# A hybrid encoder layer on one core: the output's gate row summed in the convolution stage instead of the value stage, and ones columns set by VectorE

## The chip, the cores and the metric

The kernel runs on one core of a Trainium2 chip. The metric is the device time of one execution in microseconds. The kernel before takes 1390.58 us, the median of three runs (1390.57 to 1395.54).

The core has five engines with a queue of instructions each, and each works through its queue in order: TensorE (PE, with its weight loads PEld), VectorE (DVE), ScalarE (ACT), GpSimd (POOL) and SyncE (SP). SP, ACT and POOL also issue DMAs; an issue that has to wait for a semaphore holds up what is queued behind it on that engine. SBUF is the on-chip memory; PSUM is where TensorE's results land.

## The reference, cut to what matters

One layer over 2048 tokens of width 1024, in float32:

```
shift, scale, gate = split(silu(c) @ w_ada + b_ada, 3)
h = rmsnorm(x, norm_w) * (1 + scale) + shift
proj = h @ w_in + b_in
na_out = neighbourhood_attention(q, k, v, rpb) * silu(z)
qk = silu(conv5(concat(ml_q, ml_k)) + conv_b)
hm = mlstm(qk, ml_v, forward) + mlstm(qk, ml_v, backward), gated and normalised
x = x + gate * (concat(na_out, ml_out) @ w_out)
out = rmsnorm(x, final_norm_w)
```

What the change is about is `gate`: a row of 1024 numbers, the last third of silu(c) times w_ada (1024 x 1024 of it, 4.2 MB) plus its bias. The kernel multiplies it into the columns of w_out before the output projection.

## The kernel before, in words

Every large matmul is done as three, on a high and a low part of each operand (`mm3`, lines 426 to 431), so that float32 precision is kept. The layer goes through these stages:

- **Start** (`start`): loads x, computes shift and scale, normalises and transposes x into `hhi`/`hlo`, and does the first value projections.
- **Value stage** (`tok_blocks`, after two blocks that `start` does): weight blocks 2 to 5, of 256 columns each, times 16 tiles of 128 tokens. Blocks 2 and 3 go through `vo_group`, blocks 4 and 5 through `nav_group`, in groups of four tiles. A tile is 24 matmuls into one of four PSUM banks (`pp`). VectorE adds the bias from PSUM into a staging tile (L499 for `stvo`, L464 for `stv`), which frees the bank. There are two staging tiles, used by turns; the store of one (L506, L468) is deferred by a group. In `vo_group` a column of ones stands beside each head's values; POOL sets it by a memset at the head of a group (L488).
- **Convolution stage** (`conv_blocks`): weight blocks 6 to 9, two halves each, four tiles of 512 tokens per half, so 32 tiles of 24 matmuls. ScalarE moves a tile from PSUM into `u` (L773), VectorE runs the five taps (L806, L808) one tile later, ScalarE applies Silu (L809), SP stores the result (L813), and for the keys TensorE transposes it (L819) and ScalarE copies it out (L821).
- After these come the mLSTM with the remaining projections (`phase1b`), and the neighbourhood attention with the output projection (`phase2`).

Beside the main work of a stage runs a chain of small steps, a Python generator called `self.chain`. `next(self.chain, None)` after each tile lets it issue one step.

- In the value stage the chain is `gate_chain` (the mLSTM's gates as columns), then `decays`: for 16 groups it loads rows of `d_mneg` by a broadcast (L702), POOL adds a mask (L710), ScalarE takes the exponential (L714) and stores the result into `d_ck` (L716). `decays` has a second generator, `beside`, which it steps once per group: `gate_row`.
- `gate_row` loads eight row blocks of w_ada, 128 x 1024 (512 KB) each, into the two halves of `wide` (L401), and sums them on VectorE, each row weighted by its element of silu(c), into `gsum` (L408, L410). A matmul with a column of ones adds the 128 partitions (L418), VectorE adds the bias (L420), and the row is written to DRAM, to `d_gate`. The final norm's weights go the same way, through `wide` into `d_fnw`.
- In the convolution stage the chain is `gated_out`. It reads `d_gate` back as a broadcast over 128 partitions (L730), loads w_out in 16 halves of 128 x 512 into two buffers (L737), multiplies each by the gate (L744) and stores it in `d_wo` (L745). A half takes two steps, one per tile.

SP's queue in the convolution stage carries the weight loads (L193, `raw`), the 24 copies of table rows that `tables_rows` issues at the head of each of the first three weight blocks (L551), the stores of the convolution and `gated_out`'s loads and stores.

In the phase up to the end of the mLSTM the order of the code is not the order on the engines. The instructions are put in order when the kernel is built, by dependencies, the order of the code and an estimate of durations; the order on each engine is then fixed. The trace shows it: the first table copies (L551) of the convolution stage's first block are issued at 184.7 us. Only `phase2` has an order written out by hand.

Of the kernel before, what the change touches and what calls it, by code (L numbers as in the profile page):

```python
# [62 lines left out]
class Kernel:  # L63
# [30 lines left out]
    def scratch(self):  # L94
# [9 lines left out]
        self.d_wo = d.tile([KT, P, D], F32, name="d_wo")  # L104
        self.d_fnw = d.tile([1, D], F32, name="d_fnw")
        self.d_gate = d.tile([1, D], F32, name="d_gate")
        self.d_rneg = d.tile([NH, 15, 31], F32, name="d_rneg")
# [282 lines left out]

    def gate_row(self, pool):

        nc = self.nc
        cact = pool.tile([P, KT], F32, name="cact2")
        nc.sync.dma_start(cact, self.cT)
        nc.scalar.activation(cact, cact, AF.Silu)
        acc = pool.tile([P, D], F32, name="gsum")
        buf = [self.wide[:, :D], self.wide[:, D:]]

        def load(kt):  # L400
            nc.sync.dma_start(buf[kt % 2], self.w_ada[kt * P : (kt + 1) * P, 2 * D : 3 * D])  # L401

        load(0)
        load(1)
        yield
        for kt in range(KT):
            if kt == 0:
                nc.vector.tensor_scalar(acc, buf[0], cact[:, kt : kt + 1], None, ALU.mult)  # L408
            else:
                nc.vector.scalar_tensor_tensor(acc, buf[kt % 2], cact[:, kt : kt + 1], acc, ALU.mult, ALU.add)  # L410
            if kt + 2 < KT:
                load(kt + 2)
            yield
        row = buf[0][0:1]
        nc.sync.dma_start(row, self.b_gate)
        for j in range(2):
            ps = self.sp.tile([P, GT], F32, tag="sp", name=f"gp_{j}")
            nc.tensor.matmul(ps[0:1, :], self.ones[:, 0:1], acc[:, j * GT : (j + 1) * GT], start=True, stop=True)  # L418
            yield
            nc.vector.tensor_add(row[:, j * GT : (j + 1) * GT], row[:, j * GT : (j + 1) * GT], ps[0:1, :])  # L420
        nc.sync.dma_start(self.d_gate, row)
        row = buf[1][0:1]
        nc.sync.dma_start(row, self.fnw)
        nc.sync.dma_start(self.d_fnw, row)

    def mm3(self, ps, lhi, llo, rhi, rlo):
# [58 lines left out]
    def vo_group(self, h, slot, g, first=None):  # L485
        nc = self.nc
        st = self.stage_tile(f"stvo_{h}_{g}")
        nc.gpsimd.memset(st[:, :, 128:129], 1.0)  # L488
        brow = self.brows[h % 2]
# [67 lines left out]
    def tok_blocks(self, chain_pool):  # L557
        self.wide = chain_pool.tile([P, 2 * D], F32, name="wide")
        self.chain = itertools.chain(self.gate_chain(chain_pool, self.gates), self.decays(chain_pool, self.gate_row(chain_pool)))
        order = [2, 3, 4, 5]  # L560
        self.tables_begin(chain_pool)
        for n, blk in enumerate(order):
            self.load_w(blk + 1, (blk + 1) % 2)
            if blk < 5:
                self.load_bias(blk + 1)
            for g in range(NG):
                if blk < 4:
                    self.vo_group(blk, blk % 2, g)
                else:
                    self.nav_group(blk, blk % 2, g)  # L570
            if n > 0:
                self.tables_columns(n - 1)
        for _ in self.chain:
            pass
        self.flush()
# [108 lines left out]

    def decays(self, pool, beside):

# [21 lines left out]
        for n, (h, gi) in enumerate(groups):  # L708
# [8 lines left out]
            yield  # L717
            next(beside, None)
            yield
            if n + 2 < len(groups):  # L720
                load(n + 2)
            yield
        for _ in beside:
            pass

    def gated_out(self, pool):

        nc = self.nc
        gate = pool.tile([P, D], F32, name="gate")
        nc.sync.dma_start(gate, self.d_gate.broadcast_to([P, D]))  # L730
        halves = [(k, slice(j * GT, (j + 1) * GT)) for k in range(KT) for j in range(2)]
        raws = {}

        def load(n):
            k, cs = halves[n]
            raws[n] = pool.tile([P, GT], F32, tag="wraw", bufs=2, name=f"wraw_{n}")
            nc.sync.dma_start(raws[n], self.w_out[:, k, cs])  # L737

        load(0)
        load(1)  # L740
        yield
        for n, (k, cs) in enumerate(halves):
            raw = raws.pop(n)
            nc.vector.tensor_tensor(raw, raw, gate[:, cs], ALU.mult)  # L744
# [4 lines left out]
            yield  # L749


    def conv_blocks(self, pool):
# [4 lines left out]
        for i, (blk, kind, pair) in enumerate(order):  # L757
# [445 lines left out]
    def phase2(self):  # L1203
# [426 lines left out]
```

## Time and profile before

| | |
|---|---|
| median of three runs | 1390.58 us |
| the profiled execution | 1391.12 us |
| its span, from the first instruction to the last | 1388.9 us |
| mean granted TensorE clock | 0.983 |
| TensorE busy | 1309.5 us, 94% |
| VectorE busy | 830.7 us, 60% |
| ScalarE busy | 528.2 us, 38% |
| GpSimd busy | 292.6 us, 21% |
| moved by DMA | 263.67 MB, 190 GB/s |

In the rows of the profile a group reads: line, engine, operation, the tile it writes and those it reads, shapes and count, then busy time and the mean duration in ns, then the idle time of the engine just before these instructions and who ended it. A row of the timeline has the start and the duration in us, and in brackets the idle time before it with its releaser. A row of waits has the total, the number of waits and the longest. "SPq" and "ACTq" are DMA issues. A table of stretches has the busy time of each engine in a stretch with its number of instructions, then the granted clock, the busy share of the 16 DMA engines and the rate in GB/s.

### The profile page before, as it was taken

How to read it: one execution, taken by the hardware profiler on the slowest of the kernel's cores; microseconds unless marked ns; L12 is line 12 of the kernel's file. 1: busy time of each engine (PE TensorE's matmuls, PEld its weight loads, DVE VectorE, ACT ScalarE, POOL GpSimd, SP SyncE). 2: the span in 40 equal slices, each digit the busy share in tenths (PEclk: the TensorE clock that was granted, in tenths of full speed). 3: DMA queues.
4: the chain of work that ended last, by engine and by line, in shares of the span. 5: the costliest groups of instructions: out<-in, count | busy, mean ns of one | idle time of the engine just before them, and what ended most of it. 6: DMA issues, size and time to landing. Idle time of an engine off the chain costs nothing.

```text
span 1388.9 us, 23365 instructions
## 1 busy us (share of the span) xinstructions
PE 1309.5 (94%) x8052; PEld 1126.1 (81%) x8052; DVE 830.7 (60%) x2563; ACT 528.2 (38%) x1129; POOL 292.6 (21%) x321
## 2 busy tenths in 40 slices
PE   2989998998999999999999998999998999999996
PEld 2989998898887777888878887788876888888885
DVE  6683323111355569156867877877736777777674
ACT  4642334523222323213323313333345555555551
POOL 4453212424101010001212002212402111112111
PEclk9999999999999999999999999999999999999998
DMA  9798449788457675554776878846697897876862
GB/s 319 227 299 212 122 99 237 186 201 203 120 112 205 149 194 159 170 161 141 194 209 205 246 224 228 231 134 182 181 260 221 187 220 168 204 182 171 193 160 74
DMA packets 269707, 263.67 MB, mean 190 GB/s; under 512 B 33466, under 2 KB 230074, under 8 KB 269590
## 3 DMA queue, kind: packets, MB, share of 16 engines
q1 hardware_dynamic: 178062, 186.45, 50.5%
q0 software_dynamic: 21504, 37.73, 11.0%
q10 hardware_dynamic: 70024, 38.02, 9.7%
q8 instruction: 64, 1.05, 0.3%
q14 instruction: 53, 0.43, 0.1%
HBM read 177.57 MB, written 92.72 MB: 195 GB/s over the span
## 4 chain that ended last, share of the span: by engine, by line
PE 49%; DMA 8%; DVE 4%; issue 3%; ACT 1%; POOL 1%; POOLq 0%; ACTq 0%; SPq 0%; DVEq 0%
PE pq L865 19%; PE y L1420 10%; PE pO L1383 4%; PE pT L1368 3%; DMA tab<-d_t 2%; DMA kv<-d_ck 2%; PE pi L1093 2%; PE pc L429 2%; PE px L1091 2%; PE pc L430 2%; PE pc L431 2%; PE dc L1039 1%; PE pS L1341 1%; PE pS L1340 1%; DMA d_qna<-qst 1%
## 5 line engine op out<-in xcount | busy, mean ns | idle before, releaser
L865 PE MATMUL pq<-hhi,whi_a 128*128 128x512 f32 x512 | 208.7, 408 | 1.3 <-ACT u L773 0.8
L865 PE MATMUL pq<-hlo,whi_a 128*128 128x512 f32 x512 | 209.1, 408 | 0.0
L865 PE MATMUL pq<-hhi,wlo_a 128*128 128x512 f32 x512 | 208.4, 407 | 0.5 <-DVE wlo_a L842 0.5
L1347 ACT ACTIVATE pbuf<-pbuf,mn 128x480 f32<-128x480 f32 (+5 forms) x128 | 76.4, 598 | 105.5 <-DVE mn L1346 105.3
L865 PEld LDWEIGHTS pq<-hhi,whi_a 128*128 128x128 f32 x512 | 97.5, 190 | 19.2 <-ACT u L773 1.2
L865 PEld LDWEIGHTS pq<-hhi,wlo_a 128*128 128x128 f32 x512 | 97.5, 191 | 17.7 <-DVE wlo_a L842 1.0
L865 PEld LDWEIGHTS pq<-hlo,whi_a 128*128 128x128 f32 x512 | 97.5, 190 | 16.4
L1420 PE MATMUL y<-hhi,whi_a 128*128 128x512 f32 x256 | 85.8, 404 | 3.1 <-ACT hhi L1321 2.8
L1420 PE MATMUL y<-hhi,wlo_a 128*128 128x512 f32 x256 | 84.3, 399 | 0.0
L1346 DVE CUSTOM_DVE_ANT_0 pbuf<-pS,tab 128x480 f32<-128x480 f32 (+5 forms) x128 | 65.1, 541 | 29.3 <-PE pS L1341 19.4
L839 POOL TENSOR_TENSOR wlo_a<-rawq,whi_a 128x1024 fp32r<-128x1024 f32 x20 | 48.1, 2407 | 162.9 <-ACT whi_a L838 123.2
L1115 POOL TENSOR_TENSOR hm<-hm,ck 128x128 f32<-128x128 f32 x64 | 26.4, 412 | 263.3 <-DVE hm L1114 178.5
L429 PE MATMUL pvo<-whi_b,hhi 128*128 128x256 f32 x256 | 74.7, 292 | 7.2 <-DVE stvo L499 7.2
L1023 DVE TENSOR_SCALAR wv<-kv,gtile 128x129 f32<-128x129 f32 x120 | 37.9, 323 | 63.0 <-PE dc L1039 33.3
L1096 ACT ACTIVATE num<-px,gtile 128x129 f32<-128x129 f32 x120 | 38.3, 365 | 95.1 <-PE px L1091 75.3
L431 PE MATMUL pvo<-whi_b,hlo 128*128 128x256 f32 x256 | 73.6, 288 | 0.0
L430 PE MATMUL pvo<-wlo_b,hhi 128*128 128x256 f32 x256 | 73.6, 287 | 0.0
L499 DVE TENSOR_TENSOR stvo<-pvo,brow 128x256 f32<-128x256 f32 x64 | 26.5, 420 | 73.6 <-PE pvo L431 59.8
L714 ACT ACTIVATE dec<-dec,gtile 128x128 f32<-128x128 f32 x128 | 42.0, 392 | 69.7 <-POOL dec L710 52.2
L464 DVE TENSOR_TENSOR stv<-pv,brow 128x256 f32<-128x256 f32 x32 | 12.8, 423 | 85.4 <-DMA d_vna<-stv 38.8
L1383 PE MATMUL pO<-pt,v 128*64 128x128 f32 (+3 forms) x832 | 61.3, 283 | 0.5 <-ACT pt L1370 0.5
L1368 PE MATMUL pT<-ident,pbuf 128*128 128x128 f32 (+2 forms) x416 | 59.6, 282 | 0.0
(298 smaller groups left out, 3580.2 us busy)
## 6 DMA issues: line engine op xcount, KB each, us to landing
ck<-d_ck SPq DMA_DIRECT2D x64, 384.5 KB
kv<-d_ck SPq DMA_DIRECT2D x120, 128.5 KB
rawq<-in_w_main_dram SPq DMA_DIRECT2D x28, 512.0 KB
raw<-in_w_main_dram SPq DMA_DIRECT2D x20, 512.0 KB
d_ck<-stvo SPq DMA_DIRECT2D x16, 514.0 KB
x<-in_x_dram SPq DMA_DIRECT2D x16, 512.0 KB
wada<-in_w_ada_dram SPq DMA_DIRECT2D x32, 256.0 KB
dec<-d_mneg SPq DMA_DIRECT2D x32, 256.0 KB
```

What stands on the lines that cost most here:

```text
L429: nc.tensor.matmul(ps, lhi(k), rhi(k), start=(k == 0), stop=False)
L430: nc.tensor.matmul(ps, lhi(k), rlo(k), start=False, stop=False)
L431: nc.tensor.matmul(ps, llo(k), rhi(k), start=False, stop=(k == KT - 1))
L714: nc.scalar.activation(t[:, d, o, :], t[:, d, o, :], AF.Exp, bias=self.cols["g"][:, d, h, c : c + 1])
L839: nc.gpsimd.tensor_tensor(lo[:, :, cs], raw, hi[:, :, cs].bitcast(F32), ALU.subtract)
L865: nc.tensor.matmul(patch_ps(ps) if patch else ps, w, self.htok(h, g, k, patch), start=(k == 0 and n == 0), stop=(k == KT - 1 and n == 2))
L1096: nc.scalar.activation(num[:, d, :], px[:, d, :], AF.Copy, scale=self.cols["inter"][:, d, h, c : c + 1])
L1346: nc.vector.tensor_tensor_reduce(pt[:, :nk], ps, tabs[place[u]][j][:, :nk], 1.0, 3e38, ALU.add, ALU.min, mn)
L1347: nc.scalar.activation(pt[:, :nk], pt[:, :nk], AF.Exp, bias=mn, scale=-1.0, accum_out=sums[:, j : j + 1])
L1368: nc.tensor.transpose(ps[:cs, i, :], pts[j][:, i * cs : (i + 1) * cs], self.ident)
L1383: nc.tensor.matmul(po[j * HD : (j + 1) * HD, :], v[:n, h * HD : (h + 1) * HD], pt[j][:n, i, :], start=(i == 0), stop=(i == nch - 1))
L1420: nc.tensor.matmul(y, m[:, k, :], w[k][:, cs], start=(k == 4 and n == 0), stop=(k == 3 and n == 2))
```

## The change

`gate_row` is gone, and with it `d_gate`, `d_fnw` and the argument `beside` of `decays`. Its work is in `gated_out`, in the convolution stage: the sums are taken over halves of 512 columns, first the eight row blocks of the first half, then those of the second, each piece 128 x 512 (256 KB) in the buffers of the w_out halves. After the eighth piece of a half, a matmul with a full 128 x 128 tile of ones adds the partitions and leaves the row in all 128 of them, and VectorE adds it to `gate`, which was loaded with the bias as a broadcast. Then the 16 halves of w_out are multiplied and stored as before. The chain of the convolution stage is stepped twice per tile, before and after it; a piece of the sum takes one step, a half of w_out two. The final norm's weights are read from the kernel's input. In `vo_group` the ones columns are set by VectorE.

```diff
-    def gate_row(self, pool):
...
     def vo_group(self, h, slot, g, first=None):
-        nc.gpsimd.memset(st[:, :, 128:129], 1.0)
+        nc.vector.memset(st[:, :, 128:129], 1.0)
...
     def decays(self, pool):
             yield
-            next(beside, None)
             yield
...
     def gated_out(self, pool):
+        cact = pool.tile([P, KT], F32, name="cact2")
+        nc.sync.dma_start(cact, self.cT)
+        nc.scalar.activation(cact, cact, AF.Silu)
         gate = pool.tile([P, D], F32, name="gate")
-        nc.sync.dma_start(gate, self.d_gate.broadcast_to([P, D]))
-        halves = [(k, slice(j * GT, (j + 1) * GT)) for k in range(KT) for j in range(2)]
+        nc.sync.dma_start(gate, self.b_gate.broadcast_to([P, D]))
+        columns = [slice(j * GT, (j + 1) * GT) for j in range(2)]
+        sums = [(kt, j, self.w_ada[kt * P : (kt + 1) * P, 2 * D + j * GT : 2 * D + (j + 1) * GT]) for j in range(2) for kt in range(KT)]
+        halves = [(k, j, self.w_out[:, k, cs]) for k in range(KT) for j, cs in enumerate(columns)]
+        todo = sums + halves
...
-        for n, (k, cs) in enumerate(halves):
+        for n, (k, j, _) in enumerate(todo):
             raw = raws.pop(n)
-            nc.vector.tensor_tensor(raw, raw, gate[:, cs], ALU.mult)
-            nc.sync.dma_start(self.d_wo[k][:, cs], raw)
+            cs = columns[j]
+            if n >= len(sums):
+                nc.vector.tensor_tensor(raw, raw, gate[:, cs], ALU.mult)
+                nc.sync.dma_start(self.d_wo[k][:, cs], raw)
+            elif k == 0:
+                acc = pool.tile([P, GT], F32, tag="gsum", bufs=1, name=f"gsum_{j}")
+                nc.vector.tensor_scalar(acc, raw, cact[:, k : k + 1], None, ALU.mult)
+            else:
+                nc.vector.scalar_tensor_tensor(acc, raw, cact[:, k : k + 1], acc, ALU.mult, ALU.add)
+                if k == KT - 1:
+                    ps = self.sp.tile([P, GT], F32, tag="sp", name=f"gp_{j}")
+                    nc.tensor.matmul(ps, self.ones, acc, start=True, stop=True)
+                    yield
+                    nc.vector.tensor_add(gate[:, cs], gate[:, cs], ps)
             yield
-            if n + 2 < len(halves):
-                load(n + 2)
-            yield
+            load(n + 2)
+            if n >= len(sums):
+                yield
...
     def conv_blocks(self, pool):
                 for g in range(NG):
+                    next(self.chain, None)
                     ps = self.pp.tile([P, GT], F32, tag="pp", name=f"pc_{blk}_{sub}_{g}")
...
     def phase2(self):
-            nc.sync.dma_start(fnw[0].bitcast(F32), self.d_fnw.broadcast_to([P, D]))
+            nc.sync.dma_start(fnw[0].bitcast(F32), self.fnw.broadcast_to([P, D]))
```

More of the change, by code (lines that the diff above doesn't have):

```diff
@@ L389, in start @@
         self.flush()
-    def gate_row(self, pool):
[L393 to L404, printed above, removed]
-        yield
[L406 to L424, printed above, removed]
     def mm3(self, ps, lhi, llo, rhi, rlo):
@@ L683, in gate_chain, with decays @@
             yield
-    def decays(self, pool, beside):
+    def decays(self, pool):
         nc = self.nc
@@ L722, in decays @@
             yield
-        for _ in beside:
-            pass
     def gated_out(self, pool):
         nc = self.nc
+        cact = pool.tile([P, KT], F32, name="cact2")
+        nc.sync.dma_start(cact, self.cT)
+        nc.scalar.activation(cact, cact, AF.Silu)
         gate = pool.tile([P, D], F32, name="gate")
-        nc.sync.dma_start(gate, self.d_gate.broadcast_to([P, D]))
-        halves = [(k, slice(j * GT, (j + 1) * GT)) for k in range(KT) for j in range(2)]
+        nc.sync.dma_start(gate, self.b_gate.broadcast_to([P, D]))
[3 more added lines that the diff above has]
+        todo = sums + halves
         raws = {}
         def load(n):
-            k, cs = halves[n]
-            raws[n] = pool.tile([P, GT], F32, tag="wraw", bufs=2, name=f"wraw_{n}")
-            nc.sync.dma_start(raws[n], self.w_out[:, k, cs])
+            if n < len(todo):
+                raws[n] = pool.tile([P, GT], F32, tag="wraw", bufs=2, name=f"wraw_{n}")
+                nc.sync.dma_start(raws[n], todo[n][2])
         load(0)
```

5 lines of the change are left out of this document (1 added, 4 removed).

## The prediction

> **What bounds the kernel now.** I read the page first, then the busy time by stretches, then TensorE's waits.
>
> ```profile
> span 1388.9 us, 23365 instructions
> PE 1309.5 (94%) x8052; PEld 1126.1 (81%) x8052; DVE 830.7 (60%) x2563; ACT 528.2 (38%) x1129; POOL 292.6 (21%) x321
> ```
>
> TensorE (PE) is busy for 94% of the span. A change that leaves its matmuls alone can only win or lose in the remaining 79.4 us, so what matters is where PE waits near the edit.
>
> ```profile
> core 0: us, PE busy (x) PEld busy (x) DVE busy (x) ACT busy (x) POOL busy (x), PEclk, DMA share, GB/s
> ...
> 195.00:260.00 65.00, 57.78 (x470) 57.17 (x470) 20.99 (x31) 29.25 (x55) 17.41 (x11) 0.97 0.86 211
> 260.00:320.00 60.00, 60.00 (x494) 58.01 (x493) 9.54 (x22) 25.38 (x63) 23.93 (x10) 1.00 0.77 192
> 320.00:360.00 40.00, 35.56 (x272) 35.11 (x271) 4.69 (x13) 12.58 (x34) 13.26 (x6) 0.91 0.73 192
> 360.00:410.00 50.00, 50.00 (x228) 40.65 (x227) 23.09 (x50) 12.19 (x19) 3.34 (x2) 1.00 0.41 107
> 410.00:440.00 30.00, 27.53 (x122) 21.79 (x121) 17.61 (x30) 9.77 (x15) 4.79 (x2) 0.94 0.81 207
> 440.00:478.00 38.00, 37.80 (x172) 30.57 (x172) 19.16 (x40) 9.48 (x16) 0.00 (x0) 1.00 0.65 136
> 478.00:500.00 22.00, 19.52 (x82) 15.42 (x82) 14.01 (x22) 8.29 (x12) 5.99 (x2) 0.92 0.75 197
> 500.00:560.00 60.00, 59.22 (x255) 47.74 (x254) 52.32 (x98) 17.80 (x26) 5.02 (x2) 1.00 0.68 178
> ```
>
> The value stage ends near 359 us and the convolution stage near 560 us. The columns behind POOL are the granted clock, the DMA share and the rate. The stretches that lose PE time are 195 to 260 and 320 to 360 in the value stage, and 410 to 440 and 478 to 500 in the convolution stage; each also has a clock below 1.00. PE's waits up to 600 us name the releasers:
>
> ```profile
> PE pvo L429 <- DVE stvo L499: 7.2, 3, 3.3
> PE kt L819 <- ACT acc_k L809: 5.2, 4, 2.5
> ...
> PE pv L429 <- DVE stv L464: 4.4, 1, 4.4
> ```
>
> In the value stage PE waits only for VectorE (DVE), which adds the bias and so frees one of four PSUM banks. DVE itself was held here:
>
> ```profile
> 231.34 1.28 DVE L410 SCALAR_TENSOR_TENSOR gsum<-wide,cact,gsum 128x1024 f32<-128x1024 f32 x1 [10.02 <-DMA wide<-in_w_ada_dram]
> ...
> 248.09 2.22 DVE L410 SCALAR_TENSOR_TENSOR gsum<-wide,cact,gsum 128x1024 f32<-128x1024 f32 x1 [7.68 <-DMA wide<-in_w_ada_dram]
> 250.23 1.41 DVE L499 TENSOR_TENSOR stvo<-pvo,brow 128x256 f32<-128x256 f32 x4
> ```
>
> The gate sum stood at the head of DVE's queue waiting for its 512 KB piece (10.02 and 7.68 us) while finished tiles piled up behind it: at 250.23 four additions run back to back, and PE restarts. So the 7.2 us belong to the gate row.
>
> **Part 1, the gate row leaves the value stage.** Eight sums, eight loads and their waits go from it. The price of a PE wait is more than the wait:
>
> ```profile
> 238.60 0.38 PE L429 MATMUL pvo<-whi_b,hhi 128*128 128x256 f32 x1 [2.48 <-DVE stvo L499]
> ...
> 250.70 0.39 PE L429 MATMUL pvo<-whi_b,hhi 128*128 128x256 f32 x1 [3.30 <-DVE stvo L499]
> ```
>
> ```profile
> 238.60:243.00 4.40, 4.40 (x37) 1.00 0.58 117
> ...
> 251.00:255.00 4.00, 4.00 (x23) 0.57 0.64 159
> ```
>
> After the 3.30 us wait the granted clock is 0.57 for 4.00 us, which costs 4.00 x 0.43 = 1.7 us more; after this 2.48 us wait it stays at 1.00. So this term is 7.2 + 1.7 = **8.9 us**, and I take all of it. What is late next is the staging tile's store, which the first addition of a group waits for; bounds: 8.9 if those stores land early enough, 0 if they hold DVE as long as the loads did.
>
> **Part 2, the second wait of the value stage.** At 344 us PE waits 4.4 us for the additions of a later block:
>
> ```profile
> 344.02 1.42 DVE L464 TENSOR_TENSOR stv<-pv,brow 128x256 f32<-128x256 f32 x4 [14.89 <-DMA d_vna<-stv]
> ```
>
> ```profile
> 331.94 5.49 SPq L702 DMA_DIRECT2D dec<-d_mneg  x4
> 337.52 0.38 SPq L468 DMA_DIRECT2D d_vna<-stv  x1
> ```
>
> ```profile
> 344.60:347.00 2.40, 2.40 (x11) 0.50 1.08 325
> 347.00:350.00 3.00, 3.00 (x16) 0.50 1.04 251
> ```
>
> DVE waited for the store that SyncE (SP) issued at 337.52, and SP had spent 331.94 to 337.43 on four loads of the decays. With 5.4 us at half clock behind it (2.7 us), this wait costs 4.4 + 2.7 = **7.1 us**. Is it tied to the gate row? SP's waits from 190 to 365 us say that it may be:
>
> ```profile
> SPq L702 <- DMA d_ck<-dec: 63.6, 19, 9.0
> ...
> SPq L401 <- DMA wide<-in_w_ada_dram: 7.7, 2, 5.3
> SPq L401 <- DVE stvo L499: 7.7, 4, 3.1
> ```
>
> The decays' loads are chained through their own stores (63.6 us), and SP stood another 15.4 us in front of the gate row's loads (L401), with the decays' next loads queued behind. Without these the decay chain starts its later groups earlier, by up to 15.4 us, and the store at 337.52 needs to come only some 5 us earlier for PE not to wait. Bounds: 0 and 7.1; I take 7.1, since 15.4 is well over 5.
>
> **Part 3, the ones columns.** Sixteen memsets of 128x4 leave GpSimd (POOL) for VectorE.
>
> ```profile
> L488 POOL MEMSET stvo<- 128x4 f32 x4 | 0.4, 106 | 17.1 <-DMA d_ck<-stvo 17.1
> ```
>
> At 106 ns each they are 1.7 us of DVE in the whole stage, beside 65.00 - 20.99 = 44 us of idle DVE in the stretch from 195 to 260 alone: nothing. But these four waited 17.1 us on POOL for the staging tile's last store. On DVE that wait stands in front of additions that free PSUM. Bounds: 0, since the group's first addition must wait for the same store anyhow, and the 8.9 us of part 1 given back. I take 0.
>
> **Part 4, what the convolution stage gets.** Sixteen sums over 512 columns, sixteen 256 KB loads, the load of the column vector and its Silu, two matmuls and two additions; the sixteen gate products are moved up, from one in two tiles to one in each.
>
> ```profile
> L808 DVE SCALAR_TENSOR_TENSOR acc_k<-u,cw,acc_k 128x512 f32<-128x512 f32 x64 | 45.0, 747 | 0.3
> L744 DVE TENSOR_TENSOR wraw<-wraw,gate 128x512 f32<-128x512 f32 x16 | 10.9, 684 | 0.0
> ```
>
> ```profile
> 369.94 0.69 ACT L773 ACTIVATE u<-pc,bcol 128x512 f32<-128x512 f32 x1 [4.87 <-PE pc L431]
> ...
> 375.50 0.69 ACT L773 ACTIVATE u<-pc,bcol 128x512 f32<-128x512 f32 x1 [1.46 <-PE pc L431]
> ```
>
> A tile takes 5.6 us, by two evictions that PE released. A sum has the shape and form of L808: 16 x 0.747 = 12.0 us of DVE, in the first nine or ten of 32 tiles. From 360 to 410 DVE is busy 23.09 of 50, so 26.9 us of idle cover it. The loads add 4.2 MB where the DMA share is 0.41. If that cover were gone, up to 12.0 us would reach PE by way of the transposes that follow the convolution. On SP the loads cost sixteen issues, but SP is the tight place:
>
> ```profile
> 416.93 19.71 SPq L551 DMA_DIRECT2D d_t<-d_e  x24
> ```
>
> ```profile
> 431.85 0.68 PE L819 MATMUL kt<-ident,acc_k 128*128 128x128 f32 x4 [2.31 <-ACT acc_k L809]
> ```
>
> ```profile
> 432.00:436.00 4.00, 4.00 (x14) 0.57 0.55 183
> ```
>
> When a weight block begins, SP issues 24 table copies in 19.71 us, and every store and load of the convolution stands behind them. The result is today's PE wait of 2.31 us and a clock of 0.57 for 4.00 us (1.7 us). By the code the last sums fall at the ninth tile, where the second block starts, with their loads behind these copies. The two gate matmuls are new waits on PE for DVE: each is issued right behind its last sum, where before a step lay between. Queued behind them are the next tile's 24 matmuls. I price them by the waits for the transposes, which hang on the same DVE chain: one more wait of this size, 2.31 + 1.7 = **4.0 us**. Bounds: 0 if both matmuls are ordered late enough, 22 in the rival below. The matmuls themselves are moved and not added. The Silu on ScalarE may wait for its small load, with evictions behind it; four PSUM banks of 5.6 us each cover that.
>
> One rule of the Trainium skill bears on these prices: TensorE: Matmul & The Clock Gate, Part 1, says that the clock falls to half after at least one idle window of about 3.4 us and needs about 3.4 us of work to return. By it the 2.31 us wait costs no clock, part 4 would be 2.3 and not 4.0, and the sum 1377.4. The trace differs: 0.57 after 2.31 us, and the measurement decides.
>
> **The sum** for the profiled execution, which took 1391.12 us (0.54 above the median of 1390.58): 1391.1 - 8.9 - 7.1 + 0 + 4.0 = **1379.1 us**, 0.8% faster.
>
> **The rivals.**
>
> (a) The gate row goes, but the wait at 344 us stays, because the decay chain's own 63.6 us of SP waits set it. Against it speaks that SP loses 15.4 us of other waits. 1391.1 - 8.9 + 4.0 = 1386.2.
>
> (b) The half pieces come late. Two buffers mean that a load starts only when the sum two before is done. If a 256 KB load is as slow as the 7.68 us wait shown for a 512 KB piece, a pair of sums takes 7.7 + 1.5 = 9.2 us, against one tile's 5.6 DVE falls behind by over 3 us in each of eight tiles, and I price that at four waits of 4.0 us: 1391.1 - 16.0 + 16.0 = 1391.1. For it: DVE's order is fixed, so the convolution waits with the sum. Against: no gate product (L744) ever waits in this stage (idle 0.0), with the same 256 KB. The Trainium skill speaks for this one: DMA: Bandwidth & Descriptors, Bandwidth, advises transfers of at least 1 MiB and gives 341 GB/s for 1 MB but 138 for 64 KB, so cutting the pieces in half wastes DMA time; no run here shows those rates.
>
> (c) The change does not do what it says: the memset on VectorE stands waiting for the store in place of the gate sum. Parts 1 and 2 stay as they are: 1391.1 + 4.0 = 1395.1. For it: the 17.1 us above. Against: by the code a store is issued a whole group of four tiles before its staging tile is written again.
>
> (d) Slower: the second gate matmul is ordered on PE as if the table copies took no time. PE then waits for the 19.71 us of issues and the landing of its load, some 7.7 us, less one tile of 5.6, so 21.8, and 1.7 of clock: 23.5. It decides the sign from 16 us on if parts 1 and 2 come true. With part 2 failing too: 1391.1 - 8.9 + 23.5 = 1405.7. Against: the transposes pass the same copies with waits of 2.5 us at most.
>
> **How the numbers follow.** Forecast 0.43, (a) 0.22, (b) 0.13, (c) 0.10, (d) 0.12. A measurement of this kernel can tell about 0.5% from no change, which is 7 us: under 1383.6 counts as faster, over 1397.5 as slower. Faster: most of the forecast (0.39) and of (a) the part in which the convolution stage gives nothing back, 1382.2 (0.06): 0.45. Slower: (d) and the upper ends of (b) and (c), 0.05: 0.17. The rest is 0.38. The forecast's own range is 1370 to 1387. The low end goes below 1391.1 - 16.0 = 1375.1 because the convolution's present waits (5.2 us and twice 1.7) may also shrink. The range for all cases is 1370 to 1398, which leaves out (d) and a few hundredths on each side.
>
> **What would show it.** Part 1: no wait of PE for stvo from 195 to 260 us, a clock of 1.00 there, and DVE's idle time ended by PE. Part 2: no wait of PE for L464, and SP issuing the stores of L468 soon after each group. Part 3: memset rows on DVE with little idle time in front; (c) has DVE idle there until d_ck<-stvo. Part 4: a PE wait at gp of 2 to 3 us, more than 5 us for (d); the new sums without idle time in front, idle until wraw for (b). I am wrong if PE's waits in the convolution stage, now 5.2 us, exceed 20 us, or if the value stage ends no earlier than at 359 us.

## The result, and the profile after

The changed kernel takes 1410.35 us, the median of seven runs (1403.69 to 1412.82), beside 1393.32 us for the kernel before in the same set (seven runs, 1386.39 to 1401.71). The ratio, taken over all runs of the set, is **1.0101**, with a 95% interval of 1.0075 to 1.0128 (the two medians alone would give 1.012). The changed kernel is slower by 1%, where the prediction had it 0.8% faster. A second set with the changed kernel, below, gives 1.0083 (1.0054 to 1.0112).

The profiled execution took 1412.76 us with a span of 1410.7. These are the two lines of the page that answer to those of before.

```profile
span 1410.7 us, 23354 instructions
PE 1311.8 (93%) x8052; PEld 1127.5 (80%) x8052; DVE 824.6 (58%) x2587; ACT 524.7 (37%) x1127; POOL 290.1 (21%) x305
```

The matmuls are the same 8052, and PE's busy time has grown by 2.3 us only. The span has grown by 21.8, so nearly all of it is PE standing still. Where, a table of both traces by stages shows: from 195 us to the first matmul of the nav blocks (L429 before, L392 after), from there to the first convolution tile, and from there to the first matmul of the mLSTM stage (`pq`). Columns as in the prediction. Before:

```profile
195.00:258.00 63.00, 55.78 (x453) 55.17 (x453) 20.57 (x30) 27.97 (x54) 17.41 (x11) 0.97 0.86 210
258.00:358.60 100.60, 96.16 (x774) 93.96 (x773) 14.17 (x34) 38.18 (x97) 35.79 (x16) 0.97 0.77 195
358.60:554.10 195.50, 189.58 (x834) 152.53 (x832) 120.84 (x231) 57.14 (x85) 20.54 (x8) 0.98 0.63 159
```

After:

```profile
195.00:251.70 56.70, 56.70 (x481) 56.70 (x480) 8.57 (x27) 29.64 (x56) 16.61 (x7) 1.00 0.70 159
251.70:356.50 104.80, 95.93 (x770) 95.32 (x769) 12.38 (x32) 37.74 (x97) 35.69 (x16) 0.95 0.80 189
356.50:572.10 215.60, 194.80 (x839) 155.05 (x837) 125.61 (x239) 57.35 (x85) 21.05 (x8) 0.96 0.64 161
```

The first stretch does what part 1 said: PE is busy for all of its 56.70 us at a clock of 1.00, and 6.3 us are won. The nav blocks then give 4.2 us back. The convolution stage takes 215.6 us instead of 195.5, **20.1 us more**: that is the result. The remaining 3.8 us of the 21.8 lie behind the convolution stage, where the two kernels have the same code. Of the 20.1 us, 14.9 are idle time of PE (20.8 against 5.9) and 5.2 are longer busy time: the two gate matmuls are in this stage now (2.08 and 1.02 us in the timeline), and the clock is 0.96 instead of 0.98.

PE's waits up to 640 us name the releasers (before, the lines that differ were kt 5.2, pv 4.4, and pvo for stvo 7.2):

```profile
PE kt L798 <- ACT acc_k L788: 10.3, 5, 5.2
PE pv L392 <- DVE stv L427: 8.9, 3, 6.3
...
PE pq L844 <- ACT u L752: 5.4, 1, 5.4
PE gp L721 <- DVE gsum L718: 5.1, 1, 5.1
```

There is no wait for `stvo` any more. The wait for the nav blocks' additions is still there and longer. In the convolution stage the wait for `gp` is new (5.1), the waits for the transposes have doubled (10.3), and the first projection of the mLSTM stage waits 5.4 us for ScalarE, where before it waited 0.8. New idle time: 5.1 + 5.1 + 4.6 = 14.8 of the 14.9.

The cause of the wait at the transposes stands in another engine's queue. VectorE's waits from 355 to 590 us:

```profile
DVE gate L723 <- PE gp L721: 21.3, 2, 19.8
DVE wraw L712 <- DMA wraw<-in_w_out_dram: 17.8, 7, 8.5
...
DVE gsum L718 <- DMA wraw<-in_w_ada_dram: 6.4, 4, 2.7
```

VectorE waited 21.3 us for PE to do the two gate matmuls, 19.8 of it for the second. The timeline of VectorE at that place (start, duration, instruction, in brackets the idle time before it):

```profile
450.52 0.68 DVE L712 TENSOR_TENSOR wraw<-wraw,gate 128x512 f32<-128x512 f32 x1
470.98 0.69 DVE L723 TENSOR_TENSOR gate<-gate,gp 128x512 f32<-128x512 f32 x1 [19.77 <-PE gp L721]
471.58 0.75 DVE L787 SCALAR_TENSOR_TENSOR acc_k<-u,cw,acc_k 128x512 f32<-128x512 f32 x1
```

Of ScalarE, and of TensorE:

```profile
475.35 0.72 ACT L788 ACTIVATE acc_k<-acc_k,cb 128x512 f32<-128x512 f32 x1 [20.09 <-DVE acc_k L787]
```

```profile
469.69 0.40 PE L394 MATMUL pc<-hhi,wlo_a 128*128 128x512 f32 x1
469.92 1.02 PE L721 MATMUL gp<-gsum,ones 128*128 128x512 f32 x2
476.13 1.12 PE L798 MATMUL kt<-ident,acc_k 128*128 128x128 f32 x4 [5.19 <-ACT acc_k L788]
```

Read it as one chain. The last sum of the second half was done at 449.4 us (in the timeline, L718 at 448.67 for 0.75). The order fixed when the kernel was built had put the gate matmul behind the 18th tile on PE, of which 14 were done by then, and the addition that needs it behind the beginning of the 11th group of taps on VectorE, where VectorE already was. So VectorE came to the addition at 451 us, and PE, busy without a gap, reached the matmul at 469.92. In between the taps of the finished tiles waited behind the addition, ScalarE had nothing to apply Silu to (20.09 us), and then PE itself ran out of work: the transposes wait 5.19 us. The backlog shows in the time from the end of a tile on PE to its eviction by ScalarE: 22.6 us for the 15th tile, after 0.1 for the 14th (before, it is 0.9 us for the 15th and 12.8 at most in the whole stage). It is worked off by the 22nd tile, whose eviction starts at 511.16 us, 0.3 us after PE's end.

So the wait of 5.4 us at the first `pq`, at 572 us, is not the tail of this one. A second backlog (14.1 us at the 23rd tile) begins where the third weight block starts. SP, and after it VectorE:

```profile
501.14 15.69 SPq L514 DMA_DIRECT2D d_t<-d_e  x24
516.87 0.46 SPq L703 DMA_DIRECT2D wraw<-in_w_out_dram  x1
```

```profile
520.52 0.69 DVE L712 TENSOR_TENSOR wraw<-wraw,gate 128x512 f32<-128x512 f32 x1 [8.49 <-DMA wraw<-in_w_out_dram]
```

The load of a half of w_out stands behind the 24 table copies, and VectorE, with the taps queued behind, waits 8.49 us for it. In the kernel before, no product of the gate waits in this stage; VectorE waits 7.60 us there for a store. The sixteen sums have pushed the products towards the end of the stage, where that backlog is not worked off before `pq`: 4.7 us are left at the last tile, and none before.

### The profile page after: what moved, and what is told of

Its sections match the earlier page's. It is cut to its first block, busy times and chain, and to the rows that moved or that the text cites. A ratio compares the mean times of both kernels' runs of the same rounds, so it can differ in the third digit from the quotient of the medians.

```text
span 1410.7 us, 23354 instructions
## 1 busy us (share of the span) xinstructions
PE 1311.8 (93%) x8052; PEld 1127.5 (80%) x8052; DVE 824.6 (58%) x2587; ACT 524.7 (37%) x1127; POOL 290.1 (21%) x305
## 4 chain that ended last, share of the span: by engine, by line
PE 62%; DMA 17%; DVE 7%; issue 5%; POOL 4%; ACT 3%; SPq 2%; ACTq 0%; POOLq 0%; DVEq 0%
PE pq L844 18%; PE y L1399 11%; PE pO L1362 4%; PE pT L1347 4%; DMA kv<-d_ck 3%; DMA d_ck<-dec 2%; DMA wraw<-in_w_out_dram 2%; PE pc L394 2%; PE pc L393 2%; PE pc L392 2%; PE pvo L392 2%; PE pvo L394 2%; PE pvo L393 2%; DMA d_wo<-wraw 2%; PE pvo L445 2%
## 5 line engine op out<-in xcount | busy, mean ns | idle before, releaser
L392 PE MATMUL pvo<-whi_b,hhi 128*128 128x256 f32 x256 | 73.5, 287 | 0.0
L673 POOL TENSOR_TENSOR dec<-dec,mask 128x1024 f32<-128x1024 f32 x16 | 38.1, 2384 | 129.0 <-DMA dec<-d_mneg 99.7
```

Of the source, the lines that this page charges most:

```text
L392: nc.tensor.matmul(ps, lhi(k), rhi(k), start=(k == 0), stop=False)
```

## The experiments

All ratios are to the kernel before, run beside the kernel on the same chip, with 95% intervals. In these sets the kernel before took 1380.8 to 1381.1 us (medians), in the set of the result 1393.3; only ratios are compared, therefore. Experiments 1 to 4, 5 to 8 and 9 to 12 ran on three different chips, and across these groups too it is the ratios that count. "Conv" is the time from the first convolution tile to the first `pq` in each kernel's own profiled execution. It was 195.5 us in the kernel before, in the set of the result; in the experiments' sets the kernel before has no profile, and experiments 1 and 9, whose times do not differ from it, stand for it with 190.8 and 191.2 us.

The theory: what costs is VectorE's wait for the second gate matmul, that is, the addition's place in a fixed order. The rivals: the sums and their half-size loads, the memset on VectorE, the matmuls' own wait on PE.

**1. The memset alone, on the kernel before.**

```diff
-        nc.gpsimd.memset(st[:, :, 128:129], 1.0)
+        nc.vector.memset(st[:, :, 128:129], 1.0)
```

> The kernel before with one part of the change alone: the ones columns are set by VectorE, the gate row stays in the value stage. Theory (the loss lies in the convolution stage, where the gate addition on VectorE waits for TensorE): this part costs nothing, within 3 us of the kernel before, and no more than 2 us of new waits of TensorE for stvo or stv. Rival (the memset on VectorE stands waiting for the staging tile's store and delays the additions): 5 to 10 us slower, with idle time of VectorE before stvo until d_ck<-stvo and TensorE waits for stv over 8 us.

Measured: 1.0007 (0.9990 to 1.0024), conv 190.8 us, PE's waits for `stvo` 5.0 us. The time does not move: the memset neither costs nor gains anything that can be measured.

**2. The kernel before without the gate row** (the gate is its bias alone; the final norm's weights are read from the input, as in the changed kernel).

```diff
-        ... self.decays(chain_pool, self.gate_row(chain_pool)))
+        ... self.decays(chain_pool, iter(())))
...
-        nc.sync.dma_start(gate, self.d_gate.broadcast_to([P, D]))
+        nc.sync.dma_start(gate, self.b_gate.broadcast_to([P, D]))
...
-            nc.sync.dma_start(fnw[0].bitcast(F32), self.d_fnw.broadcast_to([P, D]))
+            nc.sync.dma_start(fnw[0].bitcast(F32), self.fnw.broadcast_to([P, D]))
```

> The kernel before without the gate row: no sums, no loads of their pieces, the gate is the bias alone (that part of the computation is left out), memset on GpSimd, the rest of the convolution stage as before. Theory (the gate row cost the value stage the 7.2 us of waits and 1.7 of clock): 7 to 11 us faster than before, no wait of TensorE for stvo, and the convolution stage as long as before (195.5 us from the first pc to the first pq) within 3 us. If the second wait of the value stage (4.4 us for stv) also hung on the gate row: 14 to 18 us faster. Rival (the staging stores hold VectorE anyhow): within 4 us of before.

Measured: **0.9909** (0.9884 to 0.9935), conv 191.4. PE's waits from 200 to 640 us:

```profile
PE pv L429 <- DVE stv L464: 5.1, 1, 5.1
PE kt L819 <- ACT acc_k L809: 2.9, 2, 2.4
PE pq L865 <- ACT u L773: 0.8, 1, 0.8
```

The wait for `stvo` is gone, so part 1 is real and worth 0.9% (9 to 16 us by the interval). But the wait for `stv` is there, with no gate row at all: part 2 was wrong. SP's waits from 190 to 365 us in this kernel:

```profile
SPq L702 <- DMA d_ck<-dec: 76.8, 17, 9.9
```

Without the gate row's 15.4 us SP waits 13.2 us longer for the decays' own stores (76.8 against 63.6). So most of the time in front of the gate row's loads seems to have been time that the decay chain would have waited anyway.

**3. The changed kernel without the two matmuls and additions** (sums and loads stay; the gate is its bias alone).

```diff
-                if k == KT - 1:
-                    ps = self.sp.tile([P, GT], F32, tag="sp", name=f"gp_{j}")
-                    nc.tensor.matmul(ps, self.ones, acc, start=True, stop=True)
-                    yield
-                    nc.vector.tensor_add(gate[:, cs], gate[:, cs], ps)
```

> The changed kernel with the sums and their loads, but without the two matmuls over the partitions and the two additions to the gate (the gate is the bias alone; that part of the computation is left out). Theory (VectorE's wait of 19.8 us for the second gate matmul, and TensorE's wait of 5.1 us for the first, make the loss): 11 to 18 us faster than the changed kernel, waits of TensorE for kt back to some 5 us and none for gp, and the convolution stage under 203 us. Rival (the sixteen sums with their 256 KB loads hold VectorE): within 5 us of the changed kernel, waits of VectorE until wraw of 15 us or more and kt waits of 10 us.

Measured: **0.9931** (0.9904 to 0.9959), conv 188.8. VectorE's waits for the pieces:

```profile
DVE wraw L712 <- DMA wraw<-in_w_out_dram: 15.3, 5, 9.0
...
DVE gsum L718 <- DMA wraw<-in_w_ada_dram: 5.8, 5, 3.1
```

Sixteen sums, sixteen loads of 256 KB and the moved products are in this kernel, and its stage is no longer than that of experiment 2. VectorE waits 5.8 us for the pieces of w_ada and 15.3 for the halves of w_out, together 21.1 and more than the 19.8 us of the changed kernel, but in ten waits with the largest 9.0 (the half of w_out behind the third block's table copies). Of this PE shows little: 0.6 us of waits at the transposes, and 2.5 us at `pq` instead of 0.8.

Between this kernel (0.9931) and the changed one (1.0083, experiment 5) lie 1.5%, 21 us, and the stages differ by as much: 188.8 us here, 209.5 there. In the traces 8.3 us of it are PE's waits at the transposes (0.6 and 8.9), 4.4 the wait for `gp` and 0.4 the wait at `pq`; the other 7.5 are longer busy time, with the gate matmuls and the lower clock in it. The order on SP differs as well: without the matmuls the last piece is loaded before nearly all of the second block's table copies (405.9 us), in the changed kernel behind them (437.6 us in its first profile). So this experiment alone does not tell the matmuls from that delay; in experiments 4 and 6 the sums end at least as late in the stage as in the changed kernel.

**4. The changed kernel with the additions seven steps after the matmuls instead of one.**

```diff
-                    yield
+                    for _ in range(7):
+                        yield
                     nc.vector.tensor_add(gate[:, cs], gate[:, cs], ps)
```

> The changed kernel with the same work, but the addition to the gate seven steps after its matmul and not one. When built, the second addition then stands behind 14 started groups of taps, with its matmul after tile 19, where the changed kernel has it behind 11 groups and after tile 18: two tiles less of waiting. Theory (the wait of VectorE for the second gate matmul is what costs): that wait falls from 19.8 to some 8 us, and 5 to 9 us come back against the changed kernel. Rival (the sums and loads): within 3 us of the changed kernel, since all of them stay.

Measured: 0.9998 (0.9969 to 1.0027), conv 199.1. The matmuls stay where they were on PE (PE still waits 4.6 us for the first), but VectorE now has 14 groups of taps ahead of the second addition:

```profile
DVE gate L724 <- PE gp L721: 9.5, 2, 8.0
```

The same work, with the wait of 19.8 us down to 8.0, is 0.9% faster than the changed kernel (experiment 5), some 12 us where 5 to 9 were expected, and PE's waits at the transposes are down from 8.9 us to 1.9. What is left against experiment 3 is 0.7%, 9 us; the first matmul's wait of 4.6 us with about 2.6 us of clock behind it (worked out from the changed kernel's trace below) would be most of it. The seven steps also move the products of w_out, and the third block's backlog is smaller here (6.2 us at the 23rd tile), so not all of the gain need come from the shorter wait.

**5. The changed kernel again, on the chip of experiments 5 to 8.** No edit.

> The changed kernel once more, beside the others on this chip. From the first comparison: 1.0% slower than before, with VectorE waiting some 20 us for the second gate matmul (the order on the engines is fixed when the kernel is built), TensorE 5 us for the first, and kt waits of 10 us. If the chip's speed of DMA sets the loss, and not the order, the ratio moves by more than 0.5% and the 20 us wait shrinks below 12.

Measured: 1.0083 (1.0054 to 1.0112), conv 209.5, VectorE's wait for `gp` the same to the tenth:

```profile
DVE gate L723 <- PE gp L721: 21.3, 2, 19.8
```

**6. The changed kernel without the second half's matmul and addition** (half the gate is its bias).

```diff
-                if k == KT - 1:
+                if k == KT - 1 and j == 0:
```

> The changed kernel without the matmul and the addition for the second half of the gate (its bias alone is used there; that part of the computation is left out). All sums, all loads and the first half's matmul and addition stay in their places (after tile 7 and behind 6 groups of taps, as in the changed kernel). Theory (the wait of VectorE for the second matmul, with the taps of four tiles behind it, is the larger part of the loss): 10 to 16 us faster than the changed kernel on this chip; the wait of TensorE for gp of some 5 us stays. Rival (the first half's matmul on TensorE, 5.1 us and its clock, is the larger part): no more than 4 us faster.

Measured: 1.0018 (0.9993 to 1.0042), 10.0 us under experiment 5 by the medians, the lower edge of what the theory expected. So the second matmul and its addition are about half of the 21 us that lie between the changed kernel and experiment 3. The conv stage of the profiled execution, though, is 207.8 us, hardly shorter. PE's waits, and one of VectorE's:

```profile
PE pc L392 <- ACT u L752: 6.4, 2, 4.7
PE gp L721 <- DVE gsum L718: 5.2, 1, 5.2
```

```profile
DVE acc_q L785 <- DMA d_ck<-acc_k: 14.6, 2, 14.0
```

Where the wait of 19.8 us was, it is given back: the 15th tile is evicted 3.2 us after its end on PE, not 22.6, and the transposes wait 1.8 us. In this execution the time is lost again later in the stage. VectorE's wait of 14.0 us ends at 502.44 us, in the third block; the store it waits for was issued at 497.39 us, behind 23 table copies that hold SP from 480.80 for 15.01 us. It is the place of the second backlog above, with a longer wait than in the changed kernel (8.49 us) or in experiment 3 (8.98). This profiled execution (1387.5 us) is one of the longer ones of its kernel (1378.55 to 1389.97), so part of this may be its own; how often a wait of 14.0 us occurs in the others is not known.

**7. The changed kernel with the memset back on GpSimd.**

```diff
-        nc.vector.memset(st[:, :, 128:129], 1.0)
+        nc.gpsimd.memset(st[:, :, 128:129], 1.0)
```

> The changed kernel with the ones columns set by GpSimd again. The orders of TensorE and of SyncE are the same as in the changed kernel when built. Theory (the memset costs nothing): within 3 us of the changed kernel on this chip. Rival (the memset on VectorE holds the value stage's additions, and the longer nav waits of 8.9 us come from it): 4 to 8 us faster than the changed kernel, and waits of TensorE for stv back under 5 us.

Measured: 1.0068 (1.0045 to 1.0091), 2.3 us under experiment 5 by the medians, with overlapping intervals; conv 209.4, the wait of 19.8 us unchanged. PE's wait for the nav blocks' additions is 4.1 us here and 5.6 in experiment 5; it varies between profiled executions, and the longer 8.9 us of the result cannot be put down to the memset. With experiment 1: the memset is not the cause of the loss.

**8. No addition on VectorE at all.** The sums are taken straight into the gate's tile, which starts as zeros with the bias in one partition; the matmul is given three steps later; ScalarE, which waits for PE's tiles anyway, copies the result back. The halves of w_out come column half by column half, so that the first do not need the second total.

```diff
-        nc.sync.dma_start(gate, self.b_gate.broadcast_to([P, D]))
+        nc.gpsimd.memset(gate, 0.0)
+        nc.sync.dma_start(gate[0:1], self.b_gate)
...
+                nc.vector.scalar_tensor_tensor(gate[:, cs], raw, cact[:, k : k + 1], gate[:, cs], ALU.mult, ALU.add)
+            if n in (10, 18):
...
+                nc.tensor.matmul(pss[i], self.ones, gate[:, columns[i]], start=True, stop=True)
+            if n in (15, 22):
...
+                nc.scalar.activation(gate[:, columns[i]], pss[i], AF.Copy)
```

> The changed kernel rearranged so that VectorE never waits for a gate matmul with work behind it: the sums are taken into the gate tile itself (zero but for the bias in one partition), the matmul over the partitions is given after two more steps, ScalarE copies its result back into the gate tile, and the halves of w_out go column half by column half, so that the second copy has seven products ahead of it. Same loads, same sixteen sums. Theory: as fast as the kernel with the additions left out, 8 to 12 us faster than before, a wait of TensorE for gp under 3 us. Rival (sums and loads cost by themselves): at most 4 us faster than before.

Measured: 0.9982 (0.9960 to 1.0004), conv 198.1. VectorE's wait for `gp` is gone, but PE still waits 4.2 us at the first matmul, after 7.8 tiles, and 3.0 us at the first `pq`:

```profile
PE gp L721 <- issue: 4.2, 1, 4.2
PE pq L845 <- ACT u L753: 3.0, 1, 3.0
```

The profile names no releaser for the first; the eighth sum ends at 388.38 us and the matmul starts at 388.47, so PE seems to have waited for the sum, as in the changed kernel. This kernel is better than the changed one, and less than was expected of it: the time falls into the rival's range (at most 4 us faster than before). The rival's cause, the sums and loads, does not agree with experiment 3. Removing VectorE's wait is not all: the early first matmul has a price of its own.

**9 to 11. The wait by itself.** On the kernel before, a matmul of the gate's tile and a copy of its result by VectorE that nobody needs are added behind one of the gate products. Only the place differs: the matmul lands on PE behind tile 12, 16 or 18, VectorE's copy behind 10 groups of taps in all three. The product is number 5, 7 or 8.

```diff
+        gsum = pool.tile([P, GT], F32, name="gsum")
...
-            yield
+            if n in (5,):
+                ps = self.sp.tile([P, GT], F32, tag="sp", name=f"gp_{n}")
+                nc.tensor.matmul(ps, self.ones, gate[:, cs], start=True, stop=True)
+                yield
+                nc.vector.tensor_copy(gsum, ps)
+            else:
+                yield
```

> The kernel before with nothing of the change but one wait: one matmul of the ones with half of the gate, and one copy of its result by VectorE into a tile that nothing reads. When built, the copy stands behind 10 started groups of taps on VectorE, and the matmul after tile 12 on TensorE. Theory (what costs is VectorE waiting for a TensorE that has several tiles to go, with taps queued behind): VectorE waits under 3 us, within 3 us of before. Rival (any such pair costs, by the wait of TensorE for VectorE or by the matmul): as slow as the next two.

> The same, but the matmul is given two products later: the copy stands in the same place, behind 10 groups of taps, and the matmul after tile 16. Theory: VectorE waits four tiles (some 23 us) longer than in the first of the three, or reaches it later by what it has in hand: 8 to 20 us, and 2 to 8 us slower than before. Rival: as the first.

> The same again with the matmul after tile 18, which is where the changed kernel has its second one, and the copy behind 10 groups of taps. Theory: VectorE waits another two tiles (some 11 us) longer than in the second of the three, kt waits of TensorE rise by 4 us or more, 6 to 14 us slower than before. Rival: as the first.

Measured:

| matmul behind tile | VectorE's wait, us | PE's waits at kt, us | conv, us | ratio (95%) |
|---|---|---|---|---|
| 12 | none | 3.2 | 191.2 | 1.0005 (0.9980 to 1.0029) |
| 16 | 11.1 | 3.1 | 192.9 | 1.0013 (0.9989 to 1.0037) |
| 18 | 22.2 | 7.1 | 197.6 | 1.0039 (1.0015 to 1.0063) |

VectorE's wait in the second and in the third kernel, and PE's in the third:

```profile
DVE gsum L751 <- PE gp L749: 11.1, 1, 11.1
```

```profile
DVE gsum L751 <- PE gp L749: 22.2, 1, 22.2
```

```profile
PE kt L826 <- ACT acc_k L816: 7.1, 3, 6.4
```

With the same instructions added, a wait of 11.1 us stays hidden and one of 22.2 us reaches PE: its waits at the transposes grow by 4 us, the stage by 6.4 us against the first of the three. So VectorE's slack there lies between 11.1 and 22.2 us, by the 4 us at some 18 (an estimate). The second was expected to be 2 to 8 us slower and shows no change; the third, expected at 6 to 14, is 5 to 6 us slower (0.39%, or by the medians). Its interval excludes no change, but by little, and overlaps those of the other two; the stage lengths and waits carry the reading. Nor is it all that the changed kernel loses: there VectorE has the sums and the waits for their pieces beside the taps, and how much of its slack these take was not measured apart.

**12. Both totals late.** As experiment 8, with both matmuls only after all sixteen sums and with idle steps of the chain around them. The second copy back follows the fifth half of w_out (`n == 20`).

```diff
...
+            if n == 20:
+                back(1)
+            if n == len(sums) - 1:
+                for _ in range(6):
+                    yield
+                total(0)
+                for _ in range(2):
+                    yield
+                back(0)
+                for _ in range(2):
+                    yield
+                total(1)
+                for _ in range(2):
+                    yield
```

> The rearranged kernel (sums in the gate tile, copy back by ScalarE, halves column half by column half) with both matmuls after all sixteen sums and six or more idle steps: when built, they stand after tiles 11 and 13 on TensorE, the first three tiles later than in the first rearrangement. Theory: no wait of TensorE for gp and none of VectorE for it, 8 to 12 us faster than before and 4 us or more faster than the first rearrangement. Rival (what is left is the loads' waits on VectorE, until wraw): as the first rearrangement, within 4 us of before.

Measured: **0.9949** (0.9931 to 0.9967), 1373.91 us beside 1380.78, conv 191.6: 7 us faster than before, a little under the 8 to 12 expected. It beats both kernels, and its stage is as long as without any sums (191.4 us in experiment 2). The idle steps move the products as well: the third block's backlog is 5.2 us at the 23rd tile here and 14.8 in experiment 8, so the place of the matmuls is not the only difference between these two. No wait of PE is left in the stage but small ones, and ScalarE waits 0.55 us for the second matmul. PE's waits, and ScalarE's copies:

```profile
PE pv L392 <- DVE stv L427: 4.7, 1, 4.7
PE kt L813 <- ACT acc_k L803: 2.4, 4, 1.0
PE pq L859 <- ACT u L767: 1.2, 1, 1.2
```

```profile
413.05 0.60 ACT L707 ACTIVATE gate<-gp 128x512 f32<-128x512 f32 x1
...
425.88 0.60 ACT L707 ACTIVATE gate<-gp 128x512 f32<-128x512 f32 x1 [0.55 <-PE gp L704]
```

## Why the prediction was wrong, point by point

- **Part 1** (8.9 us, taken in full) held. PE has no wait for `stvo` after, the clock is 1.00 from 195 to 251.7 us, and experiment 2 alone gives 0.9%. The convolution stage begins at 352.0 to 353.0 us in the four experiments that keep the gate row in the value stage (1, 9 to 11), and at 339.0 to 347.2 in the other eight. In the result's own profile 6.3 us show, and the longer nav blocks behind take 4.2 of them back.
- **Part 2** (7.1 us) failed. The wait at 344 us does not hang on the gate row: it is there at 5.1 us without it (experiment 2), at 4.7 us in the fastest kernel, and is 6.3 us at its longest in the changed one. The inference that SP's 15.4 us bring the decays forward counted waits as work: without them SP waits 13.2 us longer for the decays' own stores. Rival (a) had this right. What exactly spaces the decay chain was not tried.
- **Part 3** (0) held, by experiments 1 and 7. Rival (c) fell with it: in the changed kernel, from 195 to 260 us, the memsets wait 1.6 us for the stores and the additions behind them 17.6, and PE does not notice.
- **Part 4** (+4.0) is the step that made the sign wrong. The convolution stage lost 20.1 us in the profiled execution. Its sentence "The two gate matmuls are new waits on PE for DVE" is true of the first: PE waits 5.07 us and then runs at half clock (rows below), 5.07 + 2.6 = 7.7 us rather than 4.0. Of the second the opposite holds: PE never waits for it, **VectorE waits for PE**, 19.8 us, because the matmul stands behind more than three tiles of PE's queue. I had asked what is queued behind the matmul on PE, and not what is queued behind the addition on VectorE: the taps that feed the transposes. The prediction costed VectorE by its idle time ("26.9 us of idle cover it"), which agrees with experiment 3 for the sums and says nothing of a wait that stops an engine working in order. It also took the places from the code, the last sum at the ninth tile; in the order on the engines the last sum comes after 14 tiles and its matmul after 18. That the products move to the end of the stage, behind the third block's table copies, was put at nothing; it is part of the 5.4 us at `pq`.
- The **sign of being wrong**, waits of PE over 20 us in the convolution stage, is met if the wait at `pq` is counted (20.8 us; 15.4 without it). The value stage did end earlier, at 356.5 us.
- **Rival (b)**, late half pieces, is not borne out: in experiment 3 VectorE waits 5.8 us for the pieces and 15.3 for the halves of w_out, in portions that its slack mostly takes.
- **Rival (d)** had the sign, the matmul and nearly the time (1405.7), with the wrong mechanism: the time is luck. It has PE waiting 21.8 us behind the table copies; PE does not wait for the second matmul at all. What it shares with what happened is that an order fixed beforehand decides, and that the last piece is loaded behind the copies.

The clock is what makes the waits dearer than they are. PE after three of its waits in the changed kernel, from the timeline:

```profile
400.82 2.08 PE L721 MATMUL gp<-gsum,ones 128*128 128x512 f32 x2 [5.07 <-DVE gsum L718]
```

```profile
497.71 0.66 PE L798 MATMUL kt<-ident,acc_k 128*128 128x128 f32 x4 [2.55 <-ACT acc_k L788]
```

```profile
572.06 0.80 PE L844 MATMUL pq<-hhi,whi_a 128*128 128x512 f32 x1 [5.41 <-ACT u L752]
```

And the stretches behind them (length, PE busy, granted clock, DMA share, GB/s):

```profile
400.00:404.00 4.00, 3.18 (x6) 0.50 0.48 131
...
498.00:502.00 4.00, 3.36 (x12) 0.57 0.88 227
572.00:576.00 4.00, 3.94 (x9) 0.50 0.22 66
...
404.00:406.00 2.00, 2.00 (x8) 0.50 0.00 0
```

Behind the 5.07 us wait the clock is at half for the 3.18 us that PE is busy up to 404 and for 2.00 us more: (3.18 + 2.00) x 0.5 = 2.6 us lost. Behind the wait of 2.55 us it is 0.57 (a wait of 0.64 us falls into that stretch too), as in the prediction's own row (0.57 behind 2.31 us). The Trainium skill, TensorE: Matmul & The Clock Gate, Part 1, puts the fall at an idle window of about 3.4 us. The rows here show falls at single waits of less than that. Taken through the whole sum, that figure would by estimate also have struck out the 1.7 us behind part 1's wait of 3.30 us, and so left the sum at 1379.1 us. The kernel before has two waits of 2.48 us: behind the one at 238.60 us the clock stays at 1.00, behind the one at 487.10 us it is 0.58 from 487 to 491 us. So the length of one wait does not decide alone.

What stays open: how often the third block's backlog is as long as in the profile of experiment 6; how the loss divides between the 19.8 us wait, the early first matmul and the moved products, beyond the sums above; the 0.4% by which the kernel without any gate row (experiment 2) is faster than experiment 12, where the intervals touch; and the 1% between the levels of the kernel before in the two groups of sets.

## What to carry to other kernels

When a small side task passes from one in-order engine to the busiest one and back, look up in both queues what stands ahead of the matmul and what stands behind the use of its result: a wait of the idle engine for the busy one costs what its slack does not take (here 11.1 us were hidden, 22.2 us not), however low its busy share is. Put the use of the result behind the engine's other work, or give it to an engine that already waits for PE's tiles. And time that one engine waits in front of an instruction need not be won by removing the instruction, when the chain behind it has waits of its own.

## What the runs showed of the hardware that was not expected

Sixteen loads of 256 KB through two buffers cost nothing that can be measured in experiment 3, though VectorE waits 5.8 us for them in all. What holds the engines up more is the block of table copies that SP issues: 15.01 us (experiment 6), 15.69 (the changed kernel) and 19.71 (before), with loads and stores queued behind it. At the start of the third block VectorE waits for one of these in each of four kernels: 7.60 us in the kernel before, 8.49 in the changed one, 8.98 in experiment 3 and 13.96 in experiment 6.
